# A float32 matmul with a subtraction: a head of three m tiles, nine VectorE pairs and a first store of m tiles 1 to 7, in place of eleven pairs and no head

## The chip, the cores and the metric

The kernel runs on one core of a Trainium2 chip. The metric is the device time of one execution in microseconds (us); it is 211.14 us for the kernel before, the median of four runs (210.97 to 211.45). Engines are named as in the profile: PE (TensorE), PEld (its weight loads), DVE (VectorE), ACT (ScalarE), POOL (GpSimd) and SP (SyncE, which here issues every transfer).

## What is computed

```python
batch, m, k, n = 16, 512, 1024, 768
x: (batch, m, k) float32;  weight: (k, n) float32;  sub_value: (batch, m, n) float32
return (np.matmul(x, weight) - sub_value).astype(np.float32)
```

All batches share the weight, so this is one product of 8192 x 1024 by 1024 x 768, minus a matrix of 8192 x 768.

## The kernel before

**Tiles.** The 8192 rows are 64 m tiles of 128 rows. Which rows make a tile is set by `SEGMENTS`: a segment of s tiles covers s x 128 neighbouring rows, and each of the 128 partitions holds s neighbouring rows, one per tile, so that a transfer of several tiles of a segment moves long pieces per partition. A tile needs 512 KB of x, 384 KB of sub_value and 384 KB of output. The weight is 3 MB in four chunks of 256 rows (`w_c`), two rows per partition and chunk.

**Path of one tile.** Its x lands in `x_ring` (16 tiles). ScalarE casts it to 16 bits (`cast`, line 335). It is then transposed in units of 32 bits, which carry two neighbouring values of k, in one of two ways. For most tiles TensorE does it: four transposes into `pt_b` (two buffers), line 353, then one copy by ScalarE into `xt_b` ("evacuation", line 360). For the pairs of tiles in `ON_DVE`, VectorE does it: sixteen 32x32-block transposes (line 380) for both tiles of the pair into `xtp_b` (one buffer for a pair). Then `matmuls` (lines 406 and 203) runs sixteen matmuls of 128x128 by 128x384, four for each of the four weight chunks, into one of three accumulators `po_b`. `finish` (line 426) lets VectorE subtract: the result goes into the place in `so_ring` (32 tiles) where the tile's sub_value lies, and from there SyncE stores it. The next tile but two needs the accumulator, so it waits for that subtraction.

**Order.** All engines' queues are written out by hand, in `Queue` objects; an instruction waits for semaphore counts that the bookkeeping gives it. SyncE issues the transfers in the order of `TRANSFERS`, where ('x', 8, 4) is tiles 8 to 11 of x, 's' is sub_value, 'o' the output, 'w' weight chunks. One that cannot go yet holds up those behind it: x waits for the casts of the tiles sixteen before, sub_value for the landed store of the tiles 32 before (or for the cast of the weight, which is staged in the last eight places of `so_ring`), a store for its subtractions.

**Start and loop.** TensorE runs 35 matmuls on zeros while nothing has landed. Tiles 0 and 1 are the first VectorE pair; one of the two is cast by VectorE. Weight comes in two transfers, of two chunks each; ScalarE casts six of its eight halves, VectorE two (`cast_w`, `W_ON_ACT`). TensorE's queue is a loop of six tiles (`emit_turns`, lines 67 to 109): it begins with a VectorE pair, has two code blocks, and is left at its middle (`CUT`) after the fourth tile's second chunk, in the eleventh round. Inside, the transposes of a tile stand as four in a row: those of tiles 2 and 3 of a round behind the third chunk of its tiles 0 and 1, those of tiles 4 and 5 together in tile 3. Casts of x run three to seven tiles ahead (`CAST_AHEAD`). VectorE's pair for tile t is transposed in pieces of six, six and four behind the subtractions of tiles t-5, t-4 and t-3 (`LEAD_TURN`, `PER`).

Of the kernel before, what the change touches and what calls it, by code (L numbers as in the profile page):

```python
# [8 lines left out]
P = 128  # L9
Q = 32  # L10
F32 = mybir.dt.float32
F16 = mybir.dt.float16

SEGMENTS = [(0, 2), (2, 6)] + [(at, 8) for at in range(8, 64, 8)]
# [3 lines left out]
TA = 2  # L18
TURN_AT = 2
IDLE = 34  # L20
LEAD_TURN = 5
CAST_AHEAD = (6, 7, 4, 4, 3, 3)
W_ON_ACT = {(0, 0), (0, 1), (1, 0), (1, 1), (2, 0), (3, 0)}
PER = 6
PERIOD, CUT = 6, (3, 2)
ON_DVE = frozenset(range(0, 64, 6))

TRANSFERS = [
    ('x', 0, 2), ('x', 2, 2), ('w', 0, 2), ('w', 2, 2), ('x', 4, 4), ('s', 0, 2), ('s', 2, 6),
    ('x', 8, 4), ('x', 12, 4), ('s', 8, 8), ('x', 16, 8), ('s', 16, 8), ('x', 24, 8),  # L30
    ('o', 0, 2), ('o', 2, 6), ('s', 24, 8), ('s', 32, 8), ('x', 32, 8), ('x', 40, 8),
    ('o', 8, 8), ('o', 16, 8), ('s', 40, 8), ('x', 48, 2), ('x', 50, 6), ('o', 24, 8),
    ('s', 48, 8), ('x', 56, 8), ('s', 56, 8), ('o', 32, 8), ('o', 40, 8), ('o', 48, 8),
    ('o', 56, 5), ('o', 61, 2), ('o', 63, 1),
# [3 lines left out]
class Queue:  # L38
# [15 lines left out]
    def emit(self, ops, bound=lambda n, sem, v: v, after=lambda n, sem: None):  # L54
        for n, (make, need, then) in enumerate(ops):
            for sem, v in need[:-1]:
                self.engine.wait_ge(sem, bound(n, sem, v))  # L57
                after(n, sem)
            ins = make()
            if need:  # L60
                sem, v = need[-1]
                ins.wait_op(sem, bound(n, sem, v), "sem-ge")
                after(n, sem)
            if then:
                ins.then_inc(*then)

    def emit_turns(self, turns, cut):

        first = turns[0]
        for one in turns:  # L70
            assert [[s.name for s, _ in n] for _, n, _ in one] == [[s.name for s, _ in n] for _, n, _ in first[: len(one)]]
        sems, firsts, grow, fixed = {}, {}, {}, set()
        for n, (_, need, _) in enumerate(first):
            for k, (sem, v) in enumerate(need):
                step = turns[1][n][1][k][1] - v
                for t, one in enumerate(turns):
                    assert n >= len(one) or one[n][1][k][1] == v + t * step
                if not step:
                    fixed.add((n, sem.name))
                    continue  # L80
                assert v > 0 and grow.setdefault(sem.name, step) == step
                sems[sem.name] = sem
                firsts.setdefault(sem.name, []).append(v)
        steps = {s: iter([b - a for a, b in zip(v, v[1:] + [v[0] + grow[s]])]) for s, v in firsts.items()}
        regs = {s: self.engine.alloc_register(f"at_{s}") for s in sems}
        for s, r in regs.items():
            self.engine.reg_mov(r, firsts[s][0])

        def bound(n, sem, v):
            return v if (n, sem.name) in fixed else regs[sem.name]  # L90

        def after(n, sem):
            if (n, sem.name) not in fixed:
                step = next(steps[sem.name])
                if step:
                    self.engine.reg_add(regs[sem.name], regs[sem.name], step)

        nc, engines = self.nc, OrderedEngineSet([self.engine.engine])
        turn = nc.alloc_registers("turn", engines=engines)
        nc.regs_mov(turn, 1)  # L100
        nc.br("turn_first", engines=engines)
        with nc.body("turn_first", valid_engines=engines):
            self.emit(first[:cut], bound, after)
            nc.br_cmp(turn, len(turns), on_true="turn_done", on_false="turn_second", comp_op="IS_EQ", engines=engines)
        with nc.body("turn_second", valid_engines=engines):
            self.emit(first[cut:], lambda n, sem, v: bound(n + cut, sem, v), lambda n, sem: after(n + cut, sem))
            nc.regs_alu(turn, turn, 1, op=mybir.AluOpType.add)
            nc.br("turn_first", engines=engines)
        nc.switch_bb("turn_done")
# [3 lines left out]
def kernel(  # L113
# [51 lines left out]
    idle_w = sbuf("idle_w", [P, P], F16)  # L165
    idle_x = sbuf("idle_x", [P, 512], F16)
# [4 lines left out]
    for name in ("ident", "idle", "w", "w_act", "cast", "both", "evac", "pair", "turn", "mul", "finish"):  # L171
        counter[name] = tc.alloc_semaphore(name)
# [11 lines left out]
    dve.add(lambda: nc.vector.memset(ones, 1.0), then=count("finish"))  # L184
    dve.add(lambda: nc.vector.memset(ident, 0.0), then=count("finish"))
    dve.add(lambda: nc.vector.tensor_tensor_scan(
        out=along, data0=ones, data1=ones, initial=0.0, op0=mybir.AluOpType.mult, op1=mybir.AluOpType.add,
    ), waits=[(counter["finish"], 1)], then=count("finish"))
    dve.add(lambda: nc.vector.transpose(across, along), waits=[(counter["finish"], 3)], then=count("ident"))  # L189
    for a in range(P // Q):  # L190
        here = slice(a * Q, (a + 1) * Q)
        dve.add(lambda here=here: nc.vector.tensor_tensor(  # L192
            out=ident[here, here], in0=along[here], in1=across[here], op=mybir.AluOpType.is_equal,
        ), waits=[(counter["ident"], 1)], then=count("ident"))
# [36 lines left out]
    of_x, of_s, of_o, w_landed = {}, {}, {}, {}  # L231
# [14 lines left out]
    def issue():  # L246
        nonlocal known
        while todo:
# [13 lines left out]
            if kind == "w":  # L262

                first = NSO - 2 * (n_c - at)
                st = so_ring[:, first : first + 2 * n].rearrange("p (c r) n -> p c r n", r=2)
                there = w_c[at : at + n].rearrange("c p r n -> p c r n")
                sem, value = lane((kind, at))
                sp.add(lambda here=st, there=there: nc.sync.dma_start(out=here, in_=there), then=(sem, 16))  # L268
                for c in range(n):
                    w_landed[at + c] = (sem, value, first + 2 * c)  # L270
# [7 lines left out]
            if kind == "x" and need:  # L278
                for name in ("cast", "both"):
                    mine = [cast_at[t][1] for t in need if cast_at[t][0] == name]  # L280
                    if mine:
                        waits.append((counter[name], max(mine)))
                        known |= {of_x[t] for t, (n_, v) in cast_at.items() if n_ == name and v <= max(mine)}
            if kind == "s":
# [3 lines left out]
                for t in span:  # L288
                    if t % NSO in staged:
                        waits.append(staged.pop(t % NSO))  # L290
# [10 lines left out]

    def cast_w(c):
        sem, value, first = w_landed[c]
        for r in range(2):
            name = "w_act" if (c, r) in W_ON_ACT else "w"
            to, from_ = w_sb[:, c, r], so_ring[:, first + r]
            if name == "w":
                dve.add(lambda to=to, from_=from_: nc.vector.tensor_copy(out=to, in_=from_), [(sem, value)], count(name))  # L308
            else:
                act.add(lambda to=to, from_=from_: nc.scalar.copy(out=to, in_=from_), [(sem, value)], count(name))  # L310
            staged[first + r] = (counter[name], so_far[name])
            w_at[c, r] = (counter[name], so_far[name])

    def cast(mi):
# [16 lines left out]
        name = "both" if first in ON_DVE else "cast"  # L331
        if mi == 1:
            dve.add(lambda to=to, from_=x_in: nc.vector.tensor_copy(out=to, in_=from_), waits, count(name))  # L333
        else:
            act.add(lambda: nc.scalar.copy(out=to, in_=x_in), waits, count(name))  # L335
        cast_at[mi] = (name, so_far[name])
# [3 lines left out]
    def transposes(mi):  # L340
        def one(c):
            def f():
                waits = []
                if c == 0:
                    b, before = take("pt", NPT, mi)
                    waits.append((counter["cast"], cast_at[mi][1]))
# [7 lines left out]
                if last:  # L354
                    turn_at[mi] = so_far["turn"]
                    waits = [(counter["turn"], turn_at[mi])]
                    d, before = take("xt", NXT, mi)
                    if before is not None:
                        waits.append((counter["mul"], mul_at[before]))
                    act.add(lambda: nc.scalar.copy(out=xt_b[:, d], in_=pt_b[:, b]), waits, count("evac"))  # L360
# [4 lines left out]
    def transposes_dve(mi):  # L365
# [4 lines left out]
        def one(n, a, b):  # L370
            def f():
                waits = []
                if n == 0:
                    d, before = take("xtp", NXTP, mi)
                    waits.append((counter["both"], cast_at[mi + 1][1]))
# [13 lines left out]
    def matmuls(mi, c):  # L389
        first = mi - mi % 2  # L390
        on_dve = first in ON_DVE
        waits = []
        if c == 0:
# [3 lines left out]
            else:  # L397
                waits.append((counter["evac"], evac_at[mi]))
            waits.append((counter["finish"], mi + 1 if before is None else finish_at[before]))
        xt = xtp_b[:, slot["xtp", first], mi - first] if on_dve else xt_b[:, slot["xt", mi]]  # L400
        po = po_b[:, slot["po", mi]]
        for r in range(2):
            if mi % PERIOD == 0:
                waits.append(w_at[c, r])
# [34 lines left out]

    def transpose_tile(mi):  # L440
# [3 lines left out]
    def on_dve(mi):  # L444
        return mi - mi % 2 in ON_DVE

    idle(IDLE)
    pe.add(lambda: loaded_matmul(po_b[:, NPO - 1, 0], idle_w, idle_x, start=True, stop=True), [(counter["ident"], made)])
    cast(0)
    cast(1)  # L450
    for f in transposes_dve(0):
        f()
    cast(2)
    cast(3)
    for c in range(n_c):
        cast_w(c)
# [75 lines left out]
```

## Time and profile before

| | us |
|---|---|
| median of four runs | 211.14 |
| the profiled execution | 211.13 |
| its span (what the profile shows) | 209.1 |
| VectorE, 64 subtractions, mean of one | 0.957 |
| VectorE, 176 block transposes, mean of one | 0.435 |
| ScalarE, casts of x / evacuations, mean of one | 1.05 / 1.013 |
| ScalarE / VectorE, one weight cast | 0.828 / 0.558 |

Granted clock of TensorE: full, mean 0.998. The profiled execution spends 2.03 us outside its span. Busy shares are averages over the whole span; what bounds a stage is read from that stage. In the groups of the profile a matmul's "mean ns" is its length from start to modelled end, and matmuls overlap, so its cost in a row of matmuls is the pitch, which the chain of waits gives (length of a piece divided by its count).

### The profile page before, as it was taken

What the parts mean: (1) busy time and instruction counts of PE and PEld (TensorE: products, weight loads), DVE (VectorE), ACT (ScalarE), POOL (GpSimd) and SP (SyncE); (2) the same over time, 40 slices, a digit from 0 to 9 for tenths busy, and PEclk for the clock granted to TensorE, in tenths of its full rate; (3) what the DMA queues carried; (4) which work ended last, traced back from release to release, by engine and by line L of the source; (5) the groups of instructions that cost most, each with busy time, mean ns of one, the idle gap of its engine ahead of it and who ended that gap; (6) DMA issues with size and microseconds to landing.
All of it is one profiled execution on the core that took longest, in us unless ns stands there. A gap on an engine that the chain in (4) does not pass through costs nothing.

```text
span 209.1 us, 2636 instructions
## 1 busy us (share of the span) xinstructions
PE 195.6 (94%) x1227; PEld 69.5 (33%) x681; DVE 139.8 (67%) x251; ACT 107.6 (51%) x112; POOL 0.9 (0%) x6
## 2 busy tenths in 40 slices
PE   6958996999899999999999999999999999999990
PEld 0003431442334334344333433424423343343420
DVE  2761679359659649929956965992993895598231
ACT  2555833773387095366277709626653752961300
POOL 1000000000000000000000000000000000000000
PEclk9999999999999999999999999999999999999999
DMA  5999999999999999999999999999999999999983
GB/s 205 424 433 422 462 414 439 450 459 397 414 483 408 359 417 448 434 445 444 426 433 426 414 447 447 393 453 428 428 451 428 433 426 418 451 423 433 428 369 149
DMA packets 5156, 87.07 MB, mean 417 GB/s; under 512 B 544, under 2 KB 544, under 8 KB 1568
## 3 DMA queue, kind: packets, MB, share of 16 engines
q1 hardware_dynamic: 5152, 87.03, 97.6%
q8 instruction: 1, 0.02, 0.0%
q14 instruction: 3, 0.02, 0.0%
HBM read 61.87 MB, written 25.17 MB: 416 GB/s over the span
## 4 chain that ended last, share of the span: by engine, by line
PE 72%; DMA 19%; DVE 3%; SPq 2%; issue 1%; DVEq 0%
PE po_b L203 65%; DMA so_ring<-in_sub_value_dram 19%; PE pt_b L353 7%; DVE xtp_b L380 2%; SPq L300 2%; DVE so_ring L426 1%; SPq L268 1%; SPq L527 0%; DVEq L57 0%; SPq L145 0%
## 5 line engine op out<-in xcount | busy, mean ns | idle before, releaser
L203 PE MATMUL po_b<-w_sb,xt_b 128*128 128x384 f16 x672 | 112.6, 326 | 0.0
L426 DVE TENSOR_TENSOR so_ring<-po_b,so_ring 128x768 f32<-128x768 f32 x64 | 61.0, 957 | 55.4 <-PE po_b L203 42.8
L380 DVE STREAM_TRANSPOSE xtp_b<-x16p_b 32x256 f32<-32x256 f32 x176 | 76.6, 435 | 3.0 <-ACT x16p_b L335 0.4
L360 ACT COPY xt_b<-pt_b 128x1024 f16<-128x1024 f16 x42 | 41.5, 1013 | 68.8 <-PE pt_b L353 67.7
L203 PE MATMUL po_b<-w_sb,xtp_b 128*128 128x384 f16 x352 | 62.7, 326 | 6.2 <-DVE xtp_b L380 5.2
L406 PEld LDWEIGHTS <-xt_b 128*128 128x128 f16 x336 | 32.9, 98 | 73.5 <-issue 73.2
L335 ACT CAST x_b<-x_ring 128x1024 f16<-128x1024 f32 x42 | 41.9, 1050 | 13.0 <-DMA x_ring<-in_x_dram 13.0
L406 PEld LDWEIGHTS <-xtp_b 128*128 128x128 f16 x176 | 17.2, 98 | 50.2 <-issue 34.2
L335 ACT CAST x16p_b<-x_ring 128x1024 f16<-128x1024 f32 x21 | 21.0, 1046 | 6.0 <-DMA x_ring<-in_x_dram 5.9
L353 PE MATMUL pt_b<-ident,x_b 128*128 128x128 f32 x168 | 23.6, 273 | 0.0
L353 PEld LDWEIGHTS pt_b<-ident,x_b 128*128 128x128 f32 x168 | 20.4, 141 | 8.0 <-issue 7.0
L203 PE MATMUL po_b<-idle_x,idle_w 128*128 128x512 f16 x35 | 10.3, 466 | 1.7 <-POOL idle_x L183 1.7
L310 ACT CAST w_sb<-so_ring 128x768 f16<-128x768 f32 x6 | 4.6, 828 | 2.5 <-DMA so_ring<-in_weight_dram 2.5
L333 DVE CAST x16p_b<-x_ring 128x1024 f16<-128x1024 f32 x1 | 0.7, 693 | 3.3 <-DMA x_ring<-in_x_dram 3.3
L308 DVE CAST w_sb<-so_ring 128x768 f16<-128x768 f32 x2 | 1.0, 558 | 1.7 <-DMA so_ring<-in_weight_dram 1.7
L335 ACT ACT_TABLE_LOAD x1 | 1.3, 1283 | 0.9 <-SPq L145 0.9
L192 DVE TENSOR_TENSOR ident<-along,across 32x32 f32<-32x32 f32 x4 | 0.7, 184 | 0.1
L184 DVE MEMSET ones<- 128x32 f32 x1 | 0.1, 85 | 1.0 <-SPq L145 1.0
L436 PEld LDWEIGHTS <-idle_w 128*128 128x128 f16 x1 | 0.1, 105 | 1.7 <-POOL idle_x L183 1.7
L183 POOL MEMSET idle_x<- 128x512 f16 x1 | 0.5, 529 | 0.0
L189 DVE STREAM_TRANSPOSE across<-along 128x32 f32<-128x32 f32 x1 | 0.2, 211 | 0.0
L182 POOL MEMSET idle_w<- 128x128 f16 x1 | 0.2, 206 | 0.5 <-SPq L145 0.5
(6 smaller groups left out, 0.8 us busy)
## 6 DMA issues: line engine op xcount, KB each, us to landing
so_ring<-in_sub_value_dram SPq DMA_DIRECT2D x7, 3072.0 KB, 31.5
x_ring<-in_x_dram SPq DMA_DIRECT2D x5, 4096.0 KB, 23.7
out_dram<-so_ring SPq DMA_DIRECT2D x6, 3072.0 KB, 30.4
x_ring<-in_x_dram SPq DMA_DIRECT2D x3, 2048.0 KB, 28.0
x_ring<-in_x_dram SPq DMA_DIRECT2D x3, 1024.0 KB, 6.8
so_ring<-in_weight_dram SPq DMA_DIRECT2D x2, 1536.0 KB, 11.8
x_ring<-in_x_dram SPq DMA_DIRECT2D x1, 3072.0 KB, 23.0
so_ring<-in_sub_value_dram SPq DMA_DIRECT2D x1, 2304.0 KB, 23.6
```

What stands on the lines that cost most here:

```text
L192: dve.add(lambda here=here: nc.vector.tensor_tensor(out=ident[here, here], in0=along[here], in1=across[here], op=mybir.AluOpType.is_equal, ...
L203: return nc.tensor.add_instruction(mybir.InstMatmult(name=nc.get_next_instruction_name(), engine=full.engine, ins=list(full.ins), outs=lis ...
L268: sp.add(lambda here=st, there=there: nc.sync.dma_start(out=here, in_=there), then=(sem, 16))
L300: sp.add(lambda here=here, there=there: nc.sync.dma_start(out=here, in_=there), waits, (sem, 16))
L308: dve.add(lambda to=to, from_=from_: nc.vector.tensor_copy(out=to, in_=from_), [(sem, value)], count(name))
L310: act.add(lambda to=to, from_=from_: nc.scalar.copy(out=to, in_=from_), [(sem, value)], count(name))
L335: act.add(lambda: nc.scalar.copy(out=to, in_=x_in), waits, count(name))
L353: pe.add(lambda: nc.tensor.transpose(words, from_, ident), waits, count("turn") if last else None)
L360: act.add(lambda: nc.scalar.copy(out=xt_b[:, d], in_=pt_b[:, b]), waits, count("evac"))
L380: dve.add(lambda: nc.vector.transpose(xt[b * Q : (b + 1) * Q, :, a * Q : (a + 1) * Q], x16[a * Q : (a + 1) * Q, :, b * Q : (b + 1) * Q],), ...
L406: pe.add(lambda weights=weights: nc.tensor.ldweights(weights, tile_position=(0, 0)), [w for w in waits if w[0] in ready])
L426: dve.add(lambda: nc.vector.tensor_tensor(out=o, in0=po[:, :, :NS], in1=o, op=mybir.AluOpType.subtract), [landed["s", mi], (counter["mul"] ...
```

## The change

The loop, the head, the set of VectorE pairs and the list of transfers are changed together.

- `ON_DVE` is nine pairs, tiles 10, 16, ..., 58, in place of eleven, tiles 0, 6, ..., 60. TensorE transposes 46 tiles instead of 42. Tiles 4 and 5 (`EARLY`) are transposed by TensorE and evacuated into the pair's buffer, so that the loop's body has the same form for them; a small GpSimd memset (`mark`) counts as their pair.
- A head ahead of the loop: tiles 0, 1 and 2 are multiplied chunk by chunk as weight lands, with short runs of matmuls on zeros between, then their last chunks, then tile 3. The weight comes in four transfers; VectorE casts all eight halves. ScalarE casts all tiles of x.
- The loop is a counted one (`Fori`) of six tiles, tiles 4 to 63, ten rounds in one code block, left at its end. In a tile whose later tile (two ahead) is TensorE's, one transpose stands behind each of the four chunks. Casts run four tiles ahead, seven for a VectorE pair.
- The first segments are of 1 and 7 tiles instead of 2 and 6, so the first stores are of tiles 1 to 7 and of tile 0. Transfers: 39 instead of 34, in the order below. sub_value 32 to 39 now stands behind x 32 to 39; sub_value 56 to 63 behind the stores of tiles 24 to 39.

```diff
-SEGMENTS = [(0, 2), (2, 6)] + [(at, 8) for at in range(8, 64, 8)]
+SEGMENTS = [(0, 1), (1, 7)] + [(at, 8) for at in range(8, 64, 8)]
...
-CAST_AHEAD = (6, 7, 4, 4, 3, 3)
-W_ON_ACT = {(0, 0), (0, 1), (1, 0), (1, 1), (2, 0), (3, 0)}
...
-PERIOD, CUT = 6, (3, 2)
-ON_DVE = frozenset(range(0, 64, 6))
+HEAD = 3
+ON_DVE = frozenset(range(10, 60, 6))
+HEAD_SLOT = None
+LOOP = (4, 6, 10)
 TRANSFERS = [
-    ('x', 0, 2), ('x', 2, 2), ('w', 0, 2), ('w', 2, 2), ('x', 4, 4), ('s', 0, 2), ('s', 2, 6),
-    ('x', 8, 4), ('x', 12, 4), ('s', 8, 8), ('x', 16, 8), ('s', 16, 8), ('x', 24, 8),
-    ('o', 0, 2), ('o', 2, 6), ('s', 24, 8), ('s', 32, 8), ('x', 32, 8), ('x', 40, 8),
-    ('o', 8, 8), ('o', 16, 8), ('s', 40, 8), ('x', 48, 2), ('x', 50, 6), ('o', 24, 8),
-    ('s', 48, 8), ('x', 56, 8), ('s', 56, 8), ('o', 32, 8), ('o', 40, 8), ('o', 48, 8),
-    ('o', 56, 5), ('o', 61, 2), ('o', 63, 1),
+    ('x', 0, 1), ('w', 0, 1), ('x', 1, 1), ('w', 1, 1), ('x', 2, 1), ('w', 2, 1),
+    ('x', 3, 2), ('w', 3, 1), ('s', 0, 1), ('x', 5, 3), ('s', 1, 3), ('x', 8, 4),
+    ('s', 4, 4), ('x', 12, 4), ('s', 8, 8), ('x', 16, 2), ('x', 18, 6), ('s', 16, 8),
+    ('x', 24, 8), ('o', 1, 7), ('o', 0, 1), ('s', 24, 8), ('x', 32, 8), ('s', 32, 8), ('x', 40, 8),
+    ('o', 8, 8), ('o', 16, 8), ('s', 40, 8), ('x', 48, 8), ('s', 48, 8), ('x', 56, 8),
+    ('o', 24, 8), ('o', 32, 8), ('s', 56, 8), ('o', 40, 8), ('o', 48, 8), ('o', 56, 5),
+    ('o', 61, 2), ('o', 63, 1),
 ]
...
-    def emit_turns(self, turns, cut):
+    def emit_loop(self, bodies):
...
+        with self.nc.Fori(0, len(bodies), engines=OrderedEngineSet([self.engine.engine]), head_slot=HEAD_SLOT):
+            self.emit(first, value=lambda sem, v: regs[sem.name], after=after)
...
+                for r in range(2):
+                    dve.add(
+                        lambda at=at, r=r, st=st: nc.vector.tensor_copy(out=w_sb[:, at, r], in_=st[:, r]),
+                        waits=[(sem, value)], then=count("w"),
+                    )
...
+                    if mi - mi % 2 == EARLY:
+                        if mi == EARLY:
+                            take("xtp", NXTP, mi)
+                        to = xtp_b[:, slot["xtp", EARLY], mi - EARLY]
...
+    idle(13)
+    cast(0)
+    transpose_tile(0)
+    idle(5)
+    matmuls(0, 0)
+    cast(1)
+    transpose_tile(1)
+    idle(4)
+    matmuls(0, 1)
+    matmuls(1, 0)
+    matmuls(1, 1)
+    cast(2)
+    transpose_tile(2)
+    idle(3)
+    matmuls(0, 2)
+    matmuls(1, 2)
+    for c in range(3):
+        matmuls(2, c)
+    cast(3)
+    transpose_tile(3)
+    for mi in range(HEAD):
+        matmuls(mi, 3)
+        finish(mi)
...
+        t = mi + TA
+        tr = transposes(t) if ahead <= t < n_mt and t - t % 2 not in ON_DVE else []
         for c in range(n_c):
-            if (mi % PERIOD, c) == CUT:
-                marks.append(len(pe.ops))
-                for t in (mi + 1, mi + 2):
-                    if t < n_mt:
-                        transpose_tile(t)
             matmuls(mi, c)
-            if c == TURN_AT and mi % PERIOD < 2:
-                transpose_tile(mi + TA)
+            if tr:
+                tr[c]()
...
-    turns = [pe.ops[a:b] for a, b in zip(marks[::2], marks[2::2] + marks[-1:])]
-    pe.emit_turns(turns, marks[1] - marks[0])
-    pe.emit(pe.ops[marks[-1] :])
+    first, size, times = LOOP
+    pe.emit(pe.ops[: marks[first]])
+    ends = [marks[first + size * n] for n in range(times + 1)]
+    pe.emit_loop([pe.ops[a:b] for a, b in zip(ends, ends[1:])])
+    pe.emit(pe.ops[ends[-1] :])
```

## The prediction

> Times are us from the start of the profiled span unless said otherwise.
>
> **What bounds the kernel now.** First the page: how full is each engine, and the DMA.
>
> ```profile
> span 209.1 us, 2636 instructions
> ...
> PE 195.6 (94%) x1227; PEld 69.5 (33%) x681; DVE 139.8 (67%) x251; ACT 107.6 (51%) x112; POOL 0.9 (0%) x6
> ...
> q1 hardware_dynamic: 5152, 87.03, 97.6%
> q8 instruction: 1, 0.02, 0.0%
> q14 instruction: 3, 0.02, 0.0%
> ```
>
> Two resources are near the whole span: TensorE and the data queue q1. So I cut the span where the chain of waits says that TensorE runs through, and read busy times by stretch (after the colon pair: length, then PE, PEld, DVE, ACT, POOL, then clock, DMA share, GB/s):
>
> ```profile
> 2.00:53.30 51.30, 45.12 (x260) 13.16 (x129) 32.45 (x65) 27.16 (x30) 0.00 (x0) 1.00 1.01 428
> 53.30:203.50 150.20, 150.19 (x968) 56.26 (x551) 105.52 (x181) 79.29 (x82) 0.00 (x0) 1.00 1.00 427
> 203.50:209.10 5.60, 0.00 (x0) 0.00 (x0) 0.96 (x1) 0.00 (x0) 0.00 (x0) 0.92 0.40 166
> ```
>
> The reader should see that the DMA share is 1.00 from 2 to 203.5, at 427 to 428 GB/s, in both stretches, also in the one where TensorE waits. TensorE is full only from 53.3 on. Then the chain of waits (start, length, what):
>
> ```profile
> 5.78 40.35 DMA so_ring<-in_sub_value_dram
> ...
> 53.28 2.11 PE po_b L203 x12
> 55.39 0.44 PE pt_b L353 x4
> ...
> 64.29 8.45 PE po_b L203 x52
> ...
> 197.64 5.87 PE po_b L203 x36
> 203.50 0.02 issue
> 203.53 0.96 DVE so_ring L426
> ```
>
> It starts with the transfer of sub_value tiles 8 to 15: issued at 5.78, landed at 5.78 + 40.35 = 46.13, because 14.68 MB stand before its 3.15 MB. After that the chain names TensorE. It does not show that the DMA is as late. For that I read the last three stores' issue and landing:
>
> ```profile
> 204.51 0.33 SPq L300 DMA_DIRECT2D out_dram<-so_ring  x1
> ...
> out_dram<-so_ring SPq DMA_DIRECT2D x1, 1920.0 KB, 8.7
> out_dram<-so_ring SPq DMA_DIRECT2D x1, 384.0 KB, 3.3
> ```
>
> The 1,920 KB store (tiles 56 to 60) is issued at 196.28 and lands at 204.99. The store before it lands, by the trace's landing records, at 200.43: the difference is 4.56 us for 1.966 MB, or 0.431 MB a us, the full rate. Tiles 61 and 62 land at 206.84 (0.786 MB in 1.85 us), tile 63 at 207.78 (0.393 MB in 0.94). So the slowest of the 16 packet engines never rests: the queue is a second bound, level with TensorE, and moving only TensorE cannot shorten the kernel. Bytes can't change, all inputs and the output cross once: 87.03 MB.
>
> **The change part by part.**
>
> *The transfers.* x goes from 12 transfers to 14, weight from 2 to 4 with the same rows, sub_value from 9 to 10, the output stays at 11. A packet's time can be read from the trace's packet records: median 121 ns for 3,072 bytes, 234 for 6,144, 309 for 8,192, 611 for 16,384, 912 for 24,576, 1213 for 32,768. That is about 8 ns plus 0.0368 ns a byte. Each engine serves 8 of the 128 partitions, so a transfer of one row each costs it 8 extra packets: 3 x 8 x 8 ns = 0.19 us, and five more end marks (a 4-byte packet takes 9 ns) 0.045 us. Sum: +0.24 us on the queue. Lower bound 0 (packets overlap), upper bound five whole gaps such as the first transfer shows, 0.95 issue to 1.96 first packet, 5 x 1.0 = 5 us, if each started on an empty queue. I take 0.24, since the queue is not empty: the back-to-back landings above show no gap. The Trainium skill ("DMA: Bandwidth & Descriptors", section "Anatomy of one DMA") gives a fixed 2.0 us per DMA, for GpSimd's path, mostly the confirmation of the last byte; in series that would be an estimated +10 us for five, while the 0.431 MB a us across two stores says it is hidden in a full queue.
>
> *Does the queue stay full?* Every new position, with the time it can be issued against the time the bytes before it are done (landings of before at equal bytes, plus 0.24). Transfers up to sub_value 8 to 15 need nothing and hold 17.83 MB, as before, so this again lands at 46.1. x 18 to 23 waits for the cast of tile 7, about 25, work until 48.5. x 24 waits for the cast of tile 15, about 55; work until 63. Output 1 to 7 and 0 want tile 7's subtraction, about 43. sub_value 32 waits for both to land, 81.8; behind them 24 to 31 of sub_value and x 32 to 39 are still in line until 98.5. x 40: cast of 31, about 96; line until 106. sub_value 40: 122.8, line until 130. sub_value 48: 130, line until 147. sub_value 56 now waits for output 24 to 31 to land, 171.3; line until 178.6. Output 56 to 60: tile 60, about 194.4; line until 200.4. Output 61 and 62: 200.1, line until 205.2; output 63: 202.7, line until 207.1. The closest has 4 us in hand, so nothing leaves the queue empty.
>
> *TensorE.* One matmul of 384 columns costs 162.5 ns (the 52 in 8.45 us), a tile of 16 costs 2.6; four transposes 0.4375 (the 0.44). Single transposes between matmul chunks cost the same, 109 each: in the trace the weight load (141 ns) hides under the matmul before it (162.5). The head lets TensorE work on tiles 0 to 2 while weight arrives. That gain is largely thrown away at sub_value 8 to 15: three accumulators mean that tile 11 needs the subtraction of tile 8, which ends at 46.13 + 0.49 + 0.96 = 47.6, the same three pieces as before. But then before has tile 12 starting only at 53.28, since VectorE's second pair stands behind that subtraction; after has pair 10 transposed ahead of it, tile 11 at 47.6, tile 12 at 50.65. From tile 11: 53 tiles x 2.6 = 137.8, transposes of tiles 13 to 63 without the eight pairs left, 35 x 0.4375 = 15.3, so 200.7. Two waits on top: 0.5 at tiles 12 to 15, whose evacuations stand on ScalarE behind the cast of tile 16 (x lands at 48.5), and 0.5 at tile 59, which needs tile 56's subtraction and so sub_value 56 to 63, now landing at 185.9 instead of 178.6. End 201.7 against 203.5: 1.8 us earlier, with four more tiles transposed (4 x 0.4375 = 1.75) already in.
>
> *VectorE, ScalarE.* Two pairs less save VectorE 32 x 435 ns = 13.9 us; six weight casts come back at 558 ns, 3.3. ScalarE loses 6 x 828 ns of weight casts and gets one x cast and four evacuations. A period of six tiles takes TensorE 17.35; VectorE needs 6 x 0.99 + 16 x 0.447 = 13.1, ScalarE 10 x 1.05 = 10.5. Cover: a third idle. Without it TensorE would wait, one for one.
>
> *The loop.* Back edges in before cost nothing: the 52 matmuls of 64.29 to 72.74 contain one (a branch at 66.84) at full pitch. Afterwards nine are taken, after a longer head, so the body lies elsewhere in the code. Bounds: 0, and 9 x 4.8 us (first x transfer, issue to landing, as the nearest fetch from memory) = 43. I take 0, by the row of before, which is the same branch on the same engine. The Trainium skill ("Runtime: NRT & Kernel Launch", "Instruction fetch mechanics") speaks against it: a taken branch whose target is outside a two-page window stalls for a fetch. It also grants TensorE a larger memory, and the row q8, one fetch in eleven rounds, shows no refetching here; by the rule at its worst the sum would rise by the 43 estimated above.
>
> **Sum.** TensorE's 1.8 us are hidden by the queue; the queue gains 0.24. Span 209.1 + 0.24 = 209.3. The profiled run took 211.13 with 209.1 in the span, 0.01 under the median of 211.14; so 211.14 + 0.24 = 211.4. I call within 0.2% (0.42 us) no change: that is about what a measurement of this kernel can tell. The four runs shown spread by 0.48.
>
> **Rivals.**
> 1. *Slower: TensorE becomes the bound.* The last store must be issued by about 204.7, so TensorE may slip 1.4 to 1.9 us. My handovers are tight in places: pair 46 is ready at 137.5 (sub_value 40 lands) + 0.45 + 4 x 0.98 + 16 x 0.447 = 149.0 for a start at 149.1 (tile 11's 47.6 counted on as above), x 48 lands at 147.2 for a transpose at 149.2. Half a us lost in each of nine periods gives 201.7 + 4.5 = 206.2, 2.7 past 203.5: 213.8. For: those margins. Against: VectorE and ScalarE are a third idle.
> 2. *Slower: code fetch on the slowest packet engine.* At 32.8 a 16 KB code packet took 0.93 us and the data packet beside it 1107 instead of 611 ns; after it the 16 landings of one transfer were 1.69 us apart instead of 0.47, at the end 2.8. TensorE's program is longer now. One more on the same engine: 0.24 + 1.43, 212.8.
> 3. *Faster: that fetch falls elsewhere or not in time to matter.* The same 1.43 us come back: 211.4 - 1.4 = 210.0. For: bytes are even over the engines and only one is late. Against: nothing in the diff moves fetches to another engine.
> 4. *The loop refetches at each back edge*: about 2.9 us (0.93 plus 2 us to start) x 9 = 26, TensorE ends at 227.8, total 235.
>
> **How the numbers follow.** Forecast 58%, own range 210.9 to 211.9; 0.36 of it within 0.2% of before (210.7 to 211.6), 0.16 above, 0.06 below. Rival 1: 10%, rival 2: 12%, rival 3: 14%, rival 4: 6%. Faster 0.06 + 0.14 = 0.20, same 0.36, slower 0.16 + 0.10 + 0.12 + 0.06 = 0.44. The range reaches from rival 3 to rival 1, 209.9 to 213.8; about 15% lies outside (rival 4, half of rival 1, a little below).
>
> **What would show it.** Sub_value 8 to 15 landing at 46.1; tile 11 at about 47.6; TensorE's last matmul at 201 to 202.5; DMA share 1.0 up to 200 and the last store landing near 208.0, some 3 us or more after issue and directly behind the one before it. Wrong if the DMA share dips, if TensorE's end is past 203.5, if more than two q8 packets appear, or if a gap stands at each back edge.

## The result and the profile after

The changed kernel takes 210.79 us (median of 36 runs, 210.39 to 211.39), the kernel before 211.17 (57 runs). The ratio is 0.9983, its 95% interval 0.9978 to 0.9987. So the time fell by 0.38 us, 0.17%: small enough for the prediction's "no change", but resolved by so many runs, and of the other sign than the forecast of +0.24. The profiled execution took 210.86 with a span of 209.04; that of before 211.13 with 209.06.

The page after, in the same lines as before: span, busy time of each engine, the DMA in 40 slices, and the queues.

```profile
span 209.0 us, 2614 instructions
...
PE 196.3 (94%) x1234; PEld 75.6 (36%) x700; DVE 128.0 (61%) x224; ACT 108.7 (52%) x113; POOL 1.0 (0%) x7
...
DMA  6999999999999999999999999999999999999992
...
q1 hardware_dynamic: 5616, 87.03, 97.8%
q8 instruction: 1, 0.02, 0.0%
q14 instruction: 3, 0.02, 0.0%
```

VectorE lost 11.8 us of work, TensorE gained 0.7, and neither moved the span. The data queue carries the same 87.03 MB in 464 packets more and is busy from the first slice to the last. One q8 and three q14 code packets are fetched, as before.

The stretches, cut where TensorE's unbroken run begins and ends (length, then PE, PEld, DVE, ACT, POOL, then granted clock, DMA share, GB/s):

```profile
2.00:45.20 43.20, 39.70 (x227) 13.07 (x124) 18.78 (x35) 23.53 (x25) 0.10 (x1) 1.00 1.01 423
45.20:201.50 156.30, 156.28 (x1008) 62.43 (x575) 107.41 (x183) 84.08 (x88) 0.00 (x0) 1.00 1.01 430
201.50:209.00 7.50, 0.00 (x0) 0.00 (x0) 0.96 (x1) 0.00 (x0) 0.00 (x0) 0.77 0.49 204
```

TensorE now runs without a pause from 45.20 instead of 53.28 and ends at 201.5 instead of 203.5. The DMA share is full in both long stretches. Pieces of the chain of waits, and the end of SyncE's and VectorE's timeline:

```profile
6.93 27.05 DMA so_ring<-in_sub_value_dram
...
44.52 0.45 DVE xtp_b L368
44.97 0.23 issue
45.20 0.81 PE po_b L198 x4
...
57.51 5.85 PE po_b L198 x36
...
74.85 5.85 PE po_b L198 x36
```

```profile
199.90 2.93 SPq L298 DMA_DIRECT2D out_dram<-so_ring  x2
...
201.52 0.96 DVE L417 TENSOR_TENSOR so_ring<-po_b,so_ring 128x768 f32<-128x768 f32 x1 [1.64 <-PE po_b L198]
```

TensorE's run now starts when VectorE has transposed pair 10 (44.52 + 0.45), no longer at tile 12 behind a second pair. The pieces of 36 matmuls at 162.5 ns recur every round with no gap. The last two stores are issued 2.0 us earlier than before. What came of it at the queue stands in the landing records (issue, and landing of the slowest of the 16 packet engines):

| transfer | before: issue, landed | after: issue, landed |
|---|---|---|
| sub_value 8 to 15 | 5.78, 46.13 | 8.19, 46.09 |
| output 48 to 55 | 182.0, 200.43 | 181.0, 200.40 |
| output 56 to 60 | 196.28, 205.00 | 194.16, 204.97 |
| output 61 and 62 | 201.91, 206.85 | 199.90, 206.80 |
| output 63 | 204.51, 207.78 | 202.50, 207.74 |

The last three issues moved by 2.0 to 2.1 us, the landings by 0.03 to 0.05. The time of the profiled run nevertheless fell by 0.27, nearly all of it outside the span. Over all runs that list a span: its mean went from 209.14 (81 runs) to 209.00 (38 runs), and the mean of time minus span from 2.07 to 1.82. So by these means 0.25 of the gain lies outside the span, where no record looks, and 0.14 inside.

### The profile page after: what moved, and what is told of

It is laid out like the page before. It is cut to its first block, busy times and chain, and to the rows that moved or that the text cites. A ratio compares the mean times of both kernels' runs of the same rounds, so it can differ in the third digit from the quotient of the medians.

```text
span 209.0 us, 2614 instructions
## 1 busy us (share of the span) xinstructions
PE 196.3 (94%) x1234; PEld 75.6 (36%) x700; DVE 128.0 (61%) x224; ACT 108.7 (52%) x113; POOL 1.0 (0%) x7
## 3 DMA queue, kind: packets, MB, share of 16 engines
q1 hardware_dynamic: 5616, 87.03, 97.8%
## 4 chain that ended last, share of the span: by engine, by line
PE 75%; DMA 13%; DVE 6%; SPq 3%; issue 1%; DVEq 0%
PE po_b L198 67%; DMA so_ring<-in_sub_value_dram 13%; PE pt_b L335 8%; DVE xtp_b L368 3%; DVE so_ring L417 2%; SPq L298 2%; SPq L262 1%; SPq L553 0%; DVEq L59 0%; SPq L138 0%
## 5 line engine op out<-in xcount | busy, mean ns | idle before, releaser
L198 PE MATMUL po_b<-w_sb,xt_b 128*128 128x384 f16 x704 | 125.9, 326 | 0.0
L348 ACT COPY xt_b<-pt_b 128x1024 f16<-128x1024 f16 x44 | 44.5, 1012 | 66.4 <-PE pt_b L335 65.4
L368 DVE STREAM_TRANSPOSE xtp_b<-x16p_b 32x256 f32<-32x256 f32 x144 | 62.7, 435 | 2.3
L317 ACT CAST x_b<-x_ring 128x1024 f16<-128x1024 f32 x46 | 47.2, 1048 | 3.7 <-DMA x_ring<-in_x_dram 3.7
L335 PE MATMUL pt_b<-ident,x_b 128*128 128x128 f32 x184 | 47.6, 274 | 1.6 <-ACT x_b L317 1.4
L335 PEld LDWEIGHTS pt_b<-ident,x_b 128*128 128x128 f32 x184 | 25.4, 141 | 46.0 <-issue 42.4
L317 ACT CAST x16p_b<-x_ring 128x1024 f16<-128x1024 f32 x18 | 18.8, 1046 | 15.5 <-DMA x_ring<-in_x_dram 15.5
L397 PEld LDWEIGHTS <-xtp_b 128*128 128x128 f16 x160 | 15.6, 98 | 20.4 <-issue 18.3
L265 DVE CAST w_sb<-so_ring 128x768 f16<-128x768 f32 x8 | 4.1, 556 | 11.3 <-DMA so_ring<-in_weight_dram 11.3
L348 ACT COPY xtp_b<-pt_b 128x1024 f16<-128x1024 f16 x2 | 2.0, 1012 | 2.1 <-PE pt_b L335 2.1
```

The source lines that it names most:

```text
L198: return nc.tensor.add_instruction(mybir.InstMatmult(name=nc.get_next_instruction_name(), engine=full.engine, ins=list(full.ins), outs=lis ...
L265: lambda at=at, r=r, st=st: nc.vector.tensor_copy(out=w_sb[:, at, r], in_=st[:, r]),
L335: pe.add(lambda: nc.tensor.transpose(words, from_, ident), waits, count("turn") if last else None)
L348: act.add(lambda: nc.scalar.copy(out=to, in_=pt_b[:, b]), waits, count("evac"))
L368: dve.add(lambda: nc.vector.transpose(xt[b * Q : (b + 1) * Q, :, a * Q : (a + 1) * Q], x16[a * Q : (a + 1) * Q, :, b * Q : (b + 1) * Q],), ...
L397: pe.add(lambda weights=weights: nc.tensor.ldweights(weights, tile_position=(0, 0)), [w for w in waits if w[0] in ready])
```

## The experiments

All ratios are to runs of the kernel before on the same chip, with 95% intervals.

### The transfers alone, and the engines alone

```diff
 kernel before
-SEGMENTS = [(0, 2), (2, 6)] + ...
+SEGMENTS = [(0, 1), (1, 7)] + ...
-TRANSFERS = [the list of before]
+TRANSFERS = [the list of after]
```

> The kernel before with the segments and the list of transfers of the changed one (39 transfers, weight in four), engines as before. Queue theory (the slowest packet engine of the one data queue sets the end, and the 0.38 us gained came with the transfers: cheaper first packets, 0.27 us, against 0.24 us for more packets): last store lands at 207.7 to 207.9, total 210.8 to 211.2. Rival (TensorE's earlier end, 201.5 instead of 203.5, gave the gain): TensorE still ends at 203.5 or, as sub_value 56 to 63 lands later, up to 1 us after that, total 211.2 to 212.2.

Measured: 212.87 (five runs), ratio 1.0088 [1.0056, 1.0120]. The page's DMA line, two stretches, and what SyncE and ScalarE do at the place of the dip:

```profile
DMA  6999999999999999999999999999699899999995
```

```profile
2.00:150.00 148.00, 141.71 (x875) 49.80 (x480) 100.00 (x180) 78.65 (x84) 0.00 (x0) 0.98 1.01 428
150.00:158.00 8.00, 7.51 (x49) 2.94 (x29) 7.76 (x16) 6.07 (x7) 0.00 (x0) 1.00 0.83 329
```

```profile
150.26 1.99 ACT L336 CAST x_b<-x_ring 128x1024 f16<-128x1024 f32 x2
```

```profile
152.32 0.33 SPq L301 DMA_DIRECT2D x_ring<-in_x_dram  x1
```

The transfer of x 56 to 63 needs the cast of tile 47. Before's casts run only three or four tiles ahead at that point of its loop, so the cast ends at 152.25 and the transfer is issued at 152.32, when the first packet engines had already run out: sub_value 48 to 55, ahead of it, lands between 151.7 and 154.62. In the kernel after the same transfer is issued at 140.24. The share falls to 0.83 and the queue has lost 1.5 us where x 56 to 63 lands (165.55 against 164.03 in the kernel after, at equal bytes), 2.2 by output 48 to 55. Neither expectation held: the new order of transfers needs the new order of casts. The time outside the span was 1.84.

```diff
 kernel after
-SEGMENTS = [(0, 1), (1, 7)] + ...
+SEGMENTS = [(0, 2), (2, 6)] + ...
-TRANSFERS = [the list of after]
+TRANSFERS = [the list of before, weight in two]
```

> The changed kernel with the segments and the list of transfers of the one before (34 transfers, weight in two), engines as changed. Queue theory: last store lands at 207.6 to 207.9 although TensorE ends well before 203.5, total 210.9 to 211.2. Rival (TensorE's end gave the gain): the whole gain stays, 210.8 or less, with the last store landing earlier than 207.5.

Measured: 215.99, ratio 1.0236 [1.0211, 1.0262]. Stretches:

```profile
2.00:62.00 60.00, 50.89 (x281) 17.47 (x157) 24.65 (x44) 29.43 (x31) 0.10 (x1) 0.94 0.99 419
62.00:68.00 6.00, 6.00 (x41) 2.35 (x23) 5.51 (x11) 2.88 (x4) 0.00 (x0) 1.00 0.93 350
...
205.00:214.60 9.60, 5.02 (x31) 1.37 (x14) 2.62 (x3) 0.92 (x1) 0.00 (x0) 1.00 0.60 252
```

Here TensorE becomes the bound. The head is written for weight in quarters; with halves, TensorE works 50.9 us of the 60 from 2 on where after's does 56.5, at a granted clock of 0.94 instead of 1.00. Its longest waits there are 4.2 us for VectorE's casts of the weight and 3.2 us for an evacuation; x 24 to 31 is issued at 61.77 instead of 54.26, which is where the DMA share falls. How much of this comes from the halved weight and how much from the rest of the list was not tried. TensorE ends at 210.0 instead of 201.5. The last store is issued 8.5 us later than after's, and the span grew by 5.6: the first 3 us were free. Both expectations missed it. The two halves of the change each lose alone; only together do they keep the queue fed.

### Is it the queue, and how much has TensorE in hand?

```diff
 kernel after
-    ('x', 24, 8), ('o', 1, 7), ('o', 0, 1), ('s', 24, 8), ...
+    ('x', 24, 8), ('o', 1, 7), ('s', 24, 8), ...
```

> The changed kernel without the store of tile 0 (that part of the output is left out): 0.393 MB less in the queue, 145 us before the end. Queue theory: the queue never empties, so all of its 0.93 us come back at the end, 209.9 (209.7 to 210.1). Rival (TensorE sets the end): nothing, 210.7 to 210.9.

Measured: 210.01, ratio 0.9940 [0.9928, 0.9953]. Against the kernel after that is 0.78 us less in the median time, 0.88 in the mean span (208.12), and 0.75 in the last landing of the profiled run (206.99); 0.393 MB at 0.431 MB a us is 0.91. A store issued at 55 us, 150 us before the end, is worth most of its queue time at the end. So the packet engine that lands last hardly rests in between.

```diff
 kernel after, in matmuls(), the first tile of every round
+                for _ in range(1 if mi >= 4 and mi % 6 == 4 and c == 0 and r == 0 and h == 0 else 0):
+                    pe.add(lambda ...: loaded_matmul(po[:, h, :NS], ..., start=True, stop=True), waits)
```

> The changed kernel with one matmul of 384 columns run once more in each round of six tiles (the first of the round's first tile, its result overwritten by the real one): 10 x 0.1625 = 1.6 us of TensorE, some of it covered by the waits around tile 11 and tile 59. Queue theory: TensorE ends at 202.5 to 203.1 instead of 201.5, still in time for the last store, total unchanged, 210.7 to 210.9. Rival (TensorE's end sets the time): +1.0 to +1.6, 211.8 to 212.4.

Measured: 210.78, ratio 0.9980 [0.9971, 0.9989]. The last store (issue; KB and us to landing):

```profile
204.01 0.33 SPq L298 DMA_DIRECT2D out_dram<-so_ring  x1
...
out_dram<-so_ring SPq DMA_DIRECT2D x1, 384.0 KB, 3.7
```

It is issued at 204.01, 1.5 us later than in the kernel after, and lands at 207.74, as there.

```diff
 the same
-                for _ in range(1 if ...
+                for _ in range(4 if ...
```

> The same with four more per round, 6.5 us of TensorE: TensorE ends at 206.2 to 207.4 and has to overrun the queue. Queue theory: the first 2.0 us (last store issued at 202.5, needed at 204.5) are free, the rest is paid: 213.4 to 214.8. Rival (TensorE's end sets the time): the whole 5 to 6 us, 215.8 to 216.8.

Measured: 213.72, ratio 1.0122 [1.0106, 1.0137]. The page's DMA line, a stretch, the timeline's end, and the last store's time to landing:

```profile
DMA  6999999999999999999999999999999999999375
```

```profile
199.00:208.40 9.40, 8.38 (x54) 2.81 (x27) 3.83 (x4) 2.02 (x2) 0.00 (x0) 1.00 0.70 295
```

```profile
207.42 0.96 DVE L422 TENSOR_TENSOR so_ring<-po_b,so_ring 128x768 f32<-128x768 f32 x1 [1.64 <-PE po_b L198]
208.40 0.33 SPq L298 DMA_DIRECT2D out_dram<-so_ring  x1
...
out_dram<-so_ring SPq DMA_DIRECT2D x1, 384.0 KB, 2.3
```

and the same store in the kernel after:

```profile
202.50 0.33 SPq L298 DMA_DIRECT2D out_dram<-so_ring  x1
...
out_dram<-so_ring SPq DMA_DIRECT2D x1, 384.0 KB, 5.2
```

Forty matmuls made the last store 5.90 us later (208.40 against 202.50), and the queue idled for a third of the last stretch. It landed at 210.67, 2.27 us after its issue, on an empty queue; in the kernel after it waits in line and needs 5.24. The landing moved by 2.93 of the 5.90, so 2.97 us had been slack. By the same 2.27, an estimate: TensorE of the kernel before could have brought its last store down at 204.51 + 2.27 = 206.78, so it had 1.0 us in hand against 207.78.

### What a packet costs

```diff
 kernel after
-    ('x', 32, 8), ('s', 32, 8), ('x', 40, 8),
+    *[('x', t, 1) for t in range(32, 40)], ('s', 32, 8), *[('x', t, 1) for t in range(40, 48)],
```

> The kernel after with x of tiles 32 to 39 and of tiles 40 to 47 each sent in eight transfers of one tile instead of one of eight: 112 packets and 14 end marks more on each packet engine, in a stretch where the queue has 10 us of work in line. Theory A (the prediction's price: 64 packets of 159 ns instead of 8 of 1213 is 0.47 us a transfer, 0.94 for both, and 14 marks of 9 ns 0.13): the last landing is 1.0 to 1.1 later, total 211.8 to 211.9. Theory B (a packet's own overhead is hidden in a full queue, which is why the change did not lose its 0.24): under 0.2 more, total 210.7 to 211.0. Theory C (each transfer costs more than its packets, as its end must be confirmed): 14 x 0.2 us or more, total over 213.

Measured: 212.14, ratio 1.0048 [1.0035, 1.0062]. The issues (KB each, median us to landing) and the queues:

```profile
x_ring<-in_x_dram SPq DMA_DIRECT2D x19, 512.0 KB, 21.2
```

```profile
q1 hardware_dynamic: 7632, 87.04, 97.8%
q14 instruction: 4, 0.03, 0.0%
```

The eight pieces of x 32 to 39 land over 9.96 us behind the transfer ahead of them, those of x 40 to 47 over 10.00. As one transfer each, in the kernel after, they take 9.73 and 9.65. So 112 packets and 14 marks cost 0.23 + 0.35 = 0.58 us, about 4.6 ns each, where the prediction's price gives 1.07. The packets' own times do add up as priced: in the mean of the 16 engines they sum to 204.37 us in the kernel after and 205.52 here, 1.15 more. Nor do the 204.37 us of the kernel after fit one behind the other between its first packet at 1.95 and the mean last landing at 205.73. So in a full queue part of a packet's time passes beside its neighbours', and a price read from single packets counts it twice. The last landing moved by 0.50 (208.24). The whole time rose by more, some 1.35 us against the kernel after. In the profiled run 0.54 of its rise of 1.04 in span lies behind the last landing: the span ends 1.83 us after it instead of 1.30, with a fourth q14 packet at 209.67 in between. The other five runs have no trace, and their mean span is 0.3 above the profiled one; that part stays open. Theory B is out, and C too, since 14 transfers cost 0.58 in the queue and not 2.8.

### The code packet

At 30.3 in the kernel after (32.8 before) the 16 KB q8 packet takes 938 ns on one packet engine, and the data packet beside it 955 instead of 460. Two edits were made against this, the first and the last of the three below; in the middle one, made for the cold start, the packet moved by accident, as it did with after's transfers, all or the first 21, on before's engines.

```diff
 kernel before
-IDLE = 34
+IDLE = 14
```

> The kernel before with 14 instead of 34 matmuls on zeros at the start, so 20 instructions fewer in TensorE's program. If the one 16 KB code packet near 32 us belongs to TensorE's program running past its first 256 instructions, and it is what makes one of the 16 packet engines late: no q8 packet, the 16 landings of one transfer stay under 0.8 us apart before 60 us, the store of tiles 48 to 55 lands 1.0 to 1.4 us before 200.43, and the total falls by 0.2 to 0.4 us only, since TensorE still ends at 203.5: 210.8 to 211.0. Rival (that packet has nothing to do with the length): q8 stays, 211.2. A colder TensorE clock at the start costs nothing by either, as TensorE waits there.

Measured: 210.88, ratio 0.9986 [0.9977, 0.9995]. The code packet is fetched at 207.9, behind the last landing; sub_value 8 to 15 lands at 44.90 instead of 46.13. But output 48 to 55 lands at 200.09, only 0.34 earlier: from x 50 to 55 on, the transfer in which a q14 packet falls at 139.8, the 16 landings are 2.2 us apart instead of 1.2. The mean span fell by 0.25 (208.86).

```diff
 kernel before
-    ('x', 0, 2), ('x', 2, 2), ...
+    ('x', 0, 1), ('x', 1, 1), ('x', 2, 2), ...
```

> The kernel before with its first x transfer cut into two of one tile each (packets of 4,096 instead of 8,192 bytes, 35 instead of 34 transfers). If small first packets shorten the cold start (the first packets of before take 0.5 to 1.1 us instead of 0.31, those of the changed kernel 0.2 to 0.4 instead of 0.16): tile 1 of x lands about 0.2 to 0.3 us before 5.77, the transfers after it 0.15 to 0.2 earlier, total 210.9 to 211.05. Rival (more packets only cost): 211.2 to 211.3.

Measured: 211.14, ratio 0.9996 [0.9987, 1.0005]. Tile 1 lands at 6.55 instead of 5.77, so smaller first packets did not shorten the cold start here. The code packet moved to 207.4, though TensorE's program is the same. Mean span 208.92, but 2.13 us outside it.

```diff
 kernel after
-    idle(13)
+    idle(1)
...
-    idle(5)
...
-    idle(4)
...
-    idle(3)
```

> The kernel after with 24 of its 25 matmuls on zeros in the head and three of their weight loads left out, so that TensorE's program is 27 instructions shorter. Theory (the last store is bound by the slowest packet engine, and the 16 KB code packet in the data stream costs that engine about half a us; TensorE has 3 us in hand): the code packet moves to a place after the last store, sub_value 8 to 15 lands with a spread under 0.8 and at about 45.1, the end is 0.2 to 0.4 earlier, total 210.4 to 210.6 and below both kernels. Rival 1 (the zero matmuls keep TensorE's clock up, and the head is late without them): granted clock of the first 30 us under 1.0, tile 11 after 47.7, total above 211. Rival 2 (the code packet's cost on one engine is taken up elsewhere before the end): total 210.7 to 210.9, as after.

Measured: 210.87, ratio 0.9974 [0.9964, 0.9984], with 211.26 for the kernel before in that job; mean span 208.96, 1.81 outside. The code packet stayed, at 29.9, and sub_value 8 to 15 landed at 46.17 with a spread of 1.86. The theory's means failed: TensorE's length alone doesn't place this packet. So what moving it would save here was not put to the test. The zero matmuls are not needed either: the granted clock of the first 30 us stays 1.00. The interval overlaps that of the kernel after, so this is no proven gain over it, and no run here gives one.

### The time outside the span

```diff
 kernel before
-    for name in ("ident", ..., "mul", "finish"):
+    for name in ("ident", ..., "mul", "finish", "spare0", "spare1"):
```

> The kernel before with two more semaphores allocated and never used; no instruction differs. The time outside the span is 2.06 us for the kernel before and 1.82 for the changed one, which has two more semaphores. If it goes with which semaphores a program has: outside 1.82, total 210.9 to 211.0. Rival (it goes with the code or the transfers): outside stays 2.06, total 211.1 to 211.2.

Measured: 211.20, ratio 1.0000 [0.9991, 1.0009], 2.07 outside. The number of semaphores is not it.

```diff
 kernel before
-    ('w', 0, 2), ('w', 2, 2),
+    ('w', 0, 1), ('w', 1, 1), ('w', 2, 1), ('w', 3, 1),
```

> The kernel before with the weight in four transfers instead of two. The same 34 transfers otherwise, 36 in all. Theory A (the 0.24 us less outside the span come with the list of transfers, and the weight's cut is the part of it): time outside the span 1.82, total 210.9 to 211.0. Theory B (they come with something else in the list or in the queues): outside 2.0 to 2.13, total 211.1 to 211.2. By the prediction's price of packets (two more end marks, and no row is cut) the span changes by less than 0.05 us in both.

Measured: 211.06, ratio 0.9989 [0.9981, 0.9998], 1.89 outside, mean span 209.16 against 209.17 in that job. Nearer to theory A: two transfers more, and 0.19 us less outside, with the span unchanged.

```diff
 kernel before, segments of after
-TRANSFERS = [the list of before]
+TRANSFERS = [after's first 21, then before's from ('s', 24, 8) on]
```

> The kernel before with the kernel after's segments and its first 21 transfers, to the stores of tiles 1 to 7 and of tile 0, and with before's own order behind them (TensorE's loop, pairs and casts as before). Theory (the cut of the start costs about 0.2 us of packets, the queue stays full, and what is saved lies outside the span): DMA share 1.00 up to 200, last landing between 207.7 and 208.0, outside 1.82, total 210.8 to 211.0. Rival (before's engines cannot feed the new start: the queue runs dry, as it did with the whole list): the DMA share dips, total over 211.5. Rival 2 (the outside part follows the order of the later transfers): outside 2.07 and total 211.1 to 211.3.

Measured: 210.92, ratio 0.9988 [0.9977, 0.9998], 1.85 outside, mean span 209.13. The queue stayed full and the time is as the theory has it, except that the last landing of the profiled run, 207.45, is a little early: the code packet is at 207.9 here too. The rival of a dry queue is out for the start; what ran dry with the whole list was the later order.

The mean of time minus span, by program:

| program | us outside the span |
|---|---|
| before; two semaphores more | 2.07; 2.07 |
| before, shorter TensorE program; first x in two | 2.03; 2.13 |
| before, weight in four | 1.89 |
| before, after's start; after's whole list | 1.85; 1.84 |
| after; shorter head; without the store of tile 0; with one, four matmuls more | 1.82; 1.81; 1.82; 1.79; 1.78 |
| after, x in single tiles | 1.78 |
| after's engines, before's list | 1.77 |

Cutting the weight brings 0.19 with before's engines. Yet after's engines have the low figure with the weight in two. So either is enough, and what they share was not found.

## Why the prediction was off, point by point

**The bound.** Right: the queue sets the end. The landings at equal bytes, the left-out store (0.75 to 0.88 of 0.91) and the added matmul (nothing) show it.

**"TensorE's 1.8 us are hidden by the queue."** Right, 2.0 us were. The single steps were less exact. Tile 11 was to start at 47.6 and tile 12 at 50.65; they started at 48.23 and 51.27, since VectorE's pair let tile 10 start only at 45.20 and TensorE then never waited for tile 8's subtraction. The two waits of 0.5 us, at tiles 12 to 15 and at tile 59, did not come. The errors cancel: 201.5 against 201.7.

**The places of the transfers.** Right: nothing is issued late, and sub_value 8 to 15 lands at 46.09. But the list of positions leaves out x 56 to 63. In the kernel after it is issued at 140.24 with work in line until 154.31; in the transfers-alone run it is the one that ran dry, by one cast. So a full queue is a property of the pair of edits.

**"The queue gains 0.24."** The first of two steps that failed, a term of the sum that was mis-sized. By the price measured under load, 4.6 ns, 24 packets and 5 marks cost 0.13: the prediction added up whole packet times, of which a full queue pays about half. The span's mean moved by -0.14 instead, 0.38 off the term, and the last landing by -0.04. So about a quarter of a us came back. Part of it shows at the start: sub_value 8 to 15, which has all 24 added packets ahead of it, lands in the mean of the 16 engines at 44.60 to 44.67 in the six traces with the new start and the code packet ahead of 36, and at 44.73 to 44.89 in the four traces with the old first transfers of x and a code packet by 36.0. With the code packet after the stores the gap is under 0.1 (44.53 and 44.59 against 44.62). What in the new start makes up for the packets, and how much of it reaches the end, is open. The slowest engine's own delays are larger than the effect: at output 48 to 55 it lands 2.0 us behind the mean of the 16 in the profile after, 2.1 before, and 0.8 to 2.3 over all traces.

**"The profiled run took 211.13 with 209.1 in the span ... so 211.14 + 0.24 = 211.4."** The second step that failed. It carries the time outside the span over to the new program without a word (2.03 us by the rounded span, 2.07 in the mean of the runs). The new program has 1.82, which is 0.25 less. Between the forecast of +0.24 and the measured -0.38 lie 0.62 us: some 0.38 of it is the queue's term, some 0.25 the time outside. The outside term alone, with the prediction's own price, would have given 211.1 and no change; with the measured price as well, 211.14 + 0.13 - 0.25 = 211.0. Why the new program has less time outside is open.

**Rival 1, TensorE becomes the bound.** It did not, and its point was set too early: the slip allowed was given as 1.4 to 1.9 us, and it was 2.97 from the new end. The step that made it so is "the last store must be issued by about 204.7": with 2.27 us from issue to landing, 205.5 is enough. The rival's mechanism is real, as the runs with four matmuls a round and with before's list show.

**Rivals 2 and 3, the code packet.** Not here: one q8 packet, at 30.3, with the same cost. The price of 1.43 us was too high for the end. Where the packet did leave the stream, the mean span fell by 0.25, 0.20 and 0.05: short TensorE program, first x in two, start alone. These are means over all runs, but where the packet fell is known for the profiled run of each program alone. What covered the rest of its loss shows in the short program's trace only, the delay at 139.8.

**Rival 4, back edges.** Wrong, as the unbroken pieces of 36 matmuls show. The 2 us to start a fetch in its price stand in no trace here. The stall that the Trainium skill ("Runtime: NRT & Kernel Launch", "Instruction fetch mechanics") gives for a branch out of the window did not appear in nine taken branches, and no second q8 packet was fetched. A round has some 190 TensorE instructions in the trace; whether any branch's target lay outside the window is not known, so the rule itself was not put to the test.

## What to carry to other kernels

When the landing records show a full queue, price an edit by its bytes, its packets and the moments at which it could run the queue dry, and find the compute engines' slack by adding known doses of work until the end moves. Test halves of a change before trusting either: here the order of transfers alone cost 0.9%, the order of the engines alone 2.4%, both together gained 0.2%. And for effects of a few tenths of a us, write down the time outside the span as a term of its own, because it belongs to the program as much as the span does.

## What the runs showed of the hardware

- The time outside the span differs by program from 1.77 to 2.13 us, and repeats for each program: 2.06 to 2.07 for the kernel before in every job.
- A transfer of 0.393 MB on an empty queue landed 2.27 us after its issue, while fourteen transfers and 112 packets more in a full queue cost 0.58 us together, though the packets' own times rose by 1.15.
- In all traces but that of the first x in two, most of the packet engines take some 0.3 to 0.9 us too long (1.2 once) for a packet of 32,768 bytes near 69.5 us, in x 24 to 31, just ahead of the first stores. In the trace of after's engines with before's list, where that transfer ran later, it comes near 72. In the nine traces with the code packet at 29.9 to 34.5, one of these packets is 1.5 to 1.7 us too long; in the four where the code packet comes after the stores, none is over 0.85 there. That the late engine suffers twice is a guess; the cause was not tried.
- The 16 KB code packet is fetched either at 29.9 to 36.0 us or at 207 to 211, and edits of the transfer list alone can switch it.
